# A hybrid block's output projection in seven products: channel tiles regrouped, two products moved forward

## Chip, cores and metric

The kernel runs on one core of one Trainium2 chip. The metric is the device time of one execution in microseconds. The kernel before takes 801.48 us, the median of three runs (801.42 to 801.86).

## What is computed

Input is x, 512 tokens by 2048 channels, in fp32. A norm and an input projection feed eight attention heads (stick-breaking weights) and eight recurrent channel groups (a scan along the tokens), each gated. Their outputs are sixteen channel tiles of 128 channels by 512 tokens, the matrix y. What the change touches is the last step:

```python
y = concat(attention * gate_a, scan * gate_r)        # (512, 2048)
out = x + y @ w_out                                   # w_out (2048, 2048)
```

## The kernel before

**Stages.** Four passes (p = 0 to 3) run three groups of the input projection each: queries and keys, the recurrent inputs, then values and attention gates (vg). Each pass finishes two heads and two recurrent groups. A finished channel tile k goes to a DRAM buffer, y_dram, by a DMA on the sync engine's queue (SP); tiles 0 to 7 are heads, 8 to 15 recurrent groups. The last four to be finished (6, 7, 14 and 15) stay in SBUF as pairs in late[k] and are multiplied out when they are needed (L566, L570). finish_vg(3, ...) is the end of the attention of heads 6 and 7.

**The output projection** is a Strassen-Winograd product. y is cut into four blocks: a11, a21 are the first and second 256 tokens of one half of the channel tiles, a12, a22 those of the other half; w_out is cut in four alike. Seven products p1 to p7 of 256 tokens by 1024 channels by 1024 columns take the place of eight. In the kernel before, the two channel halves are the even and the odd pairs: tile index k = 8b + 2a + s, where s = 0 is the first half, so that a11 holds tiles 0, 2, 4, ..., 14 and needs the late tiles 14 and 6.

**A product** (product(), L592) has two column halves m of 512 columns and, in each, four channel tiles a (two 128-channel tiles, one for each b), so eight slices. A slice takes 12 matmuls of 128x512: each fp32 operand is split into a high and a low fp32r part, and three of the four partial products are summed. The split of a weight tile is a cast on ACT (L608) and a subtraction on DVE (L609), the split of a tile of y the same (L586, L587, first half m = 0 only). The weight splits wo go through three buffers in turn, so a cast waits until the matmuls on the buffer's last contents are done.

**The weights** are four sums or single blocks of w_out, held in tiles of 512 KB. load_c (L549) loads one, as a DMA on SP's queue. add_c (L553) adds another block to a tile in place: a DMA with accum_op add on the queue of the POOL engine (the software queue q0). Both kinds, and the loads of x for the residual (load_res, L630, 256 KB, issued by ACT), run on the same 16 DMA engines. The order of products is p1, p3, p5, p7, p2, p6, p4. The set c1 is loaded, used by p1, and accumulated into after each of its splits (add_to), so that p5, p6 and p4 find the next sum there. The set c2 is loaded with one block, used by p3 as it is, accumulated into during p3, and used by p7, the fourth product. A third set, c3, is loaded for p2. s3, s5, s6 and s7 are sums of blocks of y, made on DVE; e1 is a copy of p1.

**What sets the order.** Within an engine the instructions run in a fixed order, which the tile framework's scheduler made from the program when the kernel was built; the queues of SP, ACT and POOL hold their DMAs in that order too, so an instruction that waits holds up those behind it. Each DMA also waits until an earlier DMA that used the same completion semaphore (there are eight for SP and ACT together, and eight for POOL) has landed.

Of the kernel before, what the change touches and what calls it, by code (L numbers as in the profile page):

```python
# [8 lines left out]
F32 = mybir.dt.float32  # L9
# [12 lines left out]
def hybrid_block_kernel(ctx: ExitStack, tc: tile.TileContext, x, norm_gain, w_in, q_norm_gain,  # L22
# [513 lines left out]
    for tag, cols in ((["c1_1_3", 1024], ["c1_1_2", 1024], ["c1_1_1", 1024], ["c1_1_0", 1024], ["s3", 1024],  # L536
# [3 lines left out]
        slots[tag] = cols  # L540
# [4 lines left out]
    w_out_a = w_out[0].rearrange("(b a s p) (h m n) -> s p a b h m n", p=P, s=2, a=NA, h=2, n=512)  # L545
    y_dram_a = y_dram.rearrange("(b a s) p t -> p a b s t", s=2, a=NA)
# [10 lines left out]
    ya = [held[f"ya{a}"].rearrange("p (b s t) -> p b s t", b=2, s=2) for a in range(NA)]  # L557
    c1 = {(m, a): held[f"c1_{m}_{a}"].rearrange("p (b n) -> p b n", b=2) for m in range(2) for a in range(NA)}
# [5 lines left out]
    for k in (14, 15):  # L564
        y, gate = late[k]
        nc.vector.tensor_tensor(out=ya[3][:, 1, k - 14], in0=y, in1=gate, op=ALU.mult)  # L566
    finish_vg(3, banks, wts)
    for k in (6, 7):
        y, gate = late[k]
        nc.vector.tensor_tensor(out=ya[3][:, 0, k - 6], in0=y, in1=gate, op=ALU.mult)  # L570
# [3 lines left out]
    mixer.close()
    heads.close()
    c2_pool = ctx.enter_context(tc.tile_pool(name="c2", bufs=8, reuse_waits="tile"))
    sa_pool = ctx.enter_context(tc.tile_pool(name="sa", bufs=4, reuse_waits="tile"))
    r_pool = ctx.enter_context(tc.tile_pool(name="res", bufs=4, reuse_waits="tile"))
    ps_o = ctx.enter_context(tc.tile_pool(name="ps_o", bufs=4, space=bass.MemoryType.PSUM,
                                          reuse_waits="tile"))  # L580

    def split_s(i, a, src):
        t = held.pop(f"s{a}") if i == 1 else op_tile(f"s{a}", F32R, f"os{i}_{a}")
# [6 lines left out]
    turn = iter(range(1000))  # L590

    def product(i, pool, tag, src, w, after=None):  # L592
# [4 lines left out]
        for m in range(2):  # L597
            for u in range(2):
                out[m, u] = pool.tile([P, 512], F32, tag=tag, name=f"p{i}_{m}{u}")
            for a in range(NA):  # L600
                if m == 0:
                    s.append(split_s(i, a, src[a]))
                sh, sl = s[a]
                n = next(turn)
                wt = held.pop(f"wo{n}") if n < 3 else op_tile(f"wo{n % 3}", F32R, f"wo{i}_{m}{a}")
                wt = wt.rearrange("p (x b n) -> p x b n", x=2, b=2)
                wh, wl = wt[:, 0], wt[:, 1]
                nc.scalar.copy(wh, w[m, a])  # L608
                nc.vector.tensor_tensor(out=wl, in0=w[m, a], in1=wh.bitcast(F32), op=ALU.subtract)  # L609
# [9 lines left out]
        return out  # L619

# [18 lines left out]
    def tt(out, in0, in1, op=ALU.add, eng=None):  # L639
        (eng or nc.vector).tensor_tensor(out=out, in0=in0, in1=in1, op=op)  # L640
# [4 lines left out]
    a11 = [t[:, :, 0, 0:256] for t in ya]  # L645
    a21 = [t[:, :, 0, 256:512] for t in ya]
    a12 = [t[:, :, 1, 0:256] for t in ya]
    a22 = [t[:, :, 1, 256:512] for t in ya]

    def c2_tile(name):  # L650
        return c2_pool.tile([P, 2, 512], F32, tag="c2", name=name)

    p1 = product(1, ps_mm, "mm", a11, c1, add_to(c1, 0, 1))
    c2 = {(m, a): load_c(c2_tile(f"c2_{m}_{a}"), 1, 1, m, a) for m in range(2) for a in range(NA)}
# [87 lines left out]
```

## Time and profile before

| | us |
|---|---|
| median of three runs | 801.48 (801.42, 801.48, 801.86) |
| profiled execution, its own time | 799.62 |
| its span on the core | 797.9 |
| mean granted clock | 0.987 |
| TensorE (PE) busy | 770.3 (97%) |
| DVE busy | 512.4 (64%) |
| ACT busy | 441.1 (55%) |
| POOL busy | 42.3 (5%) |

All rows below are of the profiled execution, with times from the start of its span. The output projection takes the part from 617 us on. PE busy is a share of the whole span; the stages have different limits, so the rows below are read by stage. A number in square brackets at the end of a row is the time that the engine stood idle before it, and what ended that time. Matmul ends are modelled, so starts are used here.

### The profile page before, as it was taken

How to read it: one execution, taken by the hardware profiler on the slowest of the kernel's cores; microseconds unless marked ns; L12 is line 12 of the kernel's file. 1: busy time of each engine (PE TensorE's matmuls, PEld its weight loads, DVE VectorE, ACT ScalarE, POOL GpSimd, SP SyncE). 2: the span in 40 equal slices, each digit the busy share in tenths (PEclk: the TensorE clock that was granted, in tenths of full speed). 3: DMA queues.
4: the chain of work that ended last, by engine and by line, in shares of the span. 5: the costliest groups of instructions: out<-in, count | busy, mean ns of one | idle time of the engine just before them, and what ended most of it. 6: DMA issues, size and time to landing. Idle time of an engine off the chain costs nothing.

```text
span 797.9 us, 10584 instructions
## 1 busy us (share of the span) xinstructions
PE 770.3 (97%) x3847; PEld 650.6 (82%) x3847; DVE 512.4 (64%) x857; ACT 441.1 (55%) x828; POOL 42.3 (5%) x55
## 2 busy tenths in 40 slices
PE   8999999999999999999999999999998848999997
PEld 7888889888888988888889988888987637888886
DVE  3664578782446787535478782446787916876694
ACT  5835578652356858334578752356857405454451
POOL 0000000000000000000000000000000314410220
PEclk9999999999999999999999999999999888999999
DMA  9622322233232222332322333222245999994591
GB/s 292 198 80 80 106 74 71 95 109 117 81 104 80 87 93 87 119 106 80 106 79 72 101 111 102 93 93 80 80 133 175 273 275 226 198 219 137 116 236 71
DMA packets 82680, 100.35 MB, mean 126 GB/s; under 512 B 5234, under 2 KB 61124, under 8 KB 82628
## 3 DMA queue, kind: packets, MB, share of 16 engines
q1 hardware_dynamic: 71620, 78.70, 31.2%
q0 software_dynamic: 8704, 16.78, 11.9%
q10 hardware_dynamic: 2304, 4.20, 1.5%
q8 instruction: 30, 0.49, 0.3%
q14 instruction: 22, 0.18, 0.1%
HBM read 92.32 MB, written 7.34 MB: 125 GB/s over the span
## 4 chain that ended last, share of the span: by engine, by line
PE 92%; DMA 5%; DVE 1%; issue 0%; SPq 0%; ACT 0%; DVEq 0%
PE p L616 6%; PE p L617 6%; PE p L618 6%; PE z L360 4%; DMA c<-in_w_out_dram 3%; PE qk0b L282 2%; PE qk0b L283 2%; PE xg0b L283 2%; PE qk0b L284 2%; PE xg1b L284 2%; PE xg2b L284 2%; PE xg3b L284 2%; PE xg0b L284 2%; PE xg3b L282 2%; PE xg1b L282 2%; PE xg2b L282 2%
## 5 line engine op out<-in xcount | busy, mean ns | idle before, releaser
L616 PE MATMUL p<-wo,os 128*128 128x512 f32 x192 | 67.5, 394 | 12.5 <-ACT wo L608 12.5
L617 PE MATMUL p<-wo,os 128*128 128x512 f32 x192 | 75.6, 394 | 0.0
L618 PE MATMUL p<-wo,os 128*128 128x512 f32 x192 | 75.4, 393 | 0.0
L616 PEld LDWEIGHTS p<-wo,os 128*128 128x128 f32 x192 | 36.5, 190 | 20.4 <-ACT wo L608 12.9
L608 ACT CAST wo<-c 128x1024 fp32r<-128x1024 f32 x24 | 25.2, 1050 | 45.0 <-PE p L618 29.1
L609 DVE TENSOR_TENSOR wo<-c,wo 128x1024 fp32r<-128x1024 f32 x24 | 29.4, 1224 | 32.0 <-ACT wo L608 31.9
L617 PEld LDWEIGHTS p<-wo,os 128*128 128x128 f32 x192 | 36.4, 190 | 8.3 <-DVE wo L609 0.8
L618 PEld LDWEIGHTS p<-wo,os 128*128 128x128 f32 x192 | 36.5, 190 | 7.6
L372 ACT ACTIVATE sp<-z 128x128 f32<-128x128 f32 (+3 forms) x32 | 13.9, 434 | 25.1 <-PE z L360 24.9
L283 PE MATMUL qk0b<-xl,hqk 128*128 128x512 f32 x64 | 26.4, 413 | 0.0
L284 PE MATMUL qk0b<-xh,lqk 128*128 128x512 f32 x64 | 25.2, 394 | 0.0
L283 PE MATMUL xg0b<-xl,hxg 128*128 128x512 f32 x64 | 25.2, 394 | 0.0
L282 PE MATMUL xg2b<-xh,hxg 128*128 128x512 f32 x64 | 25.1, 393 | 0.0
L282 PE MATMUL xg1b<-xh,hxg 128*128 128x512 f32 x64 | 25.1, 393 | 0.0
L282 PE MATMUL xg3b<-xh,hxg 128*128 128x512 f32 x64 | 25.1, 393 | 0.0
L282 PE MATMUL xg0b<-xh,hxg 128*128 128x512 f32 x64 | 25.1, 392 | 0.0
L283 PE MATMUL xg1b<-xl,hxg 128*128 128x512 f32 x64 | 25.1, 392 | 0.0
L283 PE MATMUL xg3b<-xl,hxg 128*128 128x512 f32 x64 | 25.1, 392 | 0.0
L283 PE MATMUL xg2b<-xl,hxg 128*128 128x512 f32 x64 | 25.1, 392 | 0.0
L284 PE MATMUL qk1b<-xh,lqk 128*128 128x512 f32 x64 | 25.0, 390 | 0.0
L282 PE MATMUL qk2b<-xh,hqk 128*128 128x512 f32 x64 | 24.9, 389 | 0.0
L282 PE MATMUL qk3b<-xh,hqk 128*128 128x512 f32 x64 | 24.9, 389 | 0.0
(538 smaller groups left out, 2440.2 us busy)
## 6 DMA issues: line engine op xcount, KB each, us to landing
c<-in_w_out_dram SPq DMA_DIRECT2D x16, 512.0 KB, 9.0
qk0r<-in_w_in_dram SPq DMA_DIRECT2D x16, 256.0 KB, 4.9
xg0r<-in_w_in_dram SPq DMA_DIRECT2D x16, 256.0 KB, 2.9
vg0r<-in_w_in_dram SPq DMA_DIRECT2D x16, 256.0 KB, 3.1
qk1r<-in_w_in_dram SPq DMA_DIRECT2D x16, 256.0 KB, 2.9
xg1r<-in_w_in_dram SPq DMA_DIRECT2D x16, 256.0 KB, 2.9
vg1r<-in_w_in_dram SPq DMA_DIRECT2D x16, 256.0 KB, 3.0
qk2r<-in_w_in_dram SPq DMA_DIRECT2D x16, 256.0 KB, 3.2
```

Source lines behind the costliest of these rows:

```text
L282: nc.tensor.matmul(banks[b], lhsT=wh[:, cs], rhs=xh[kt], start=st, stop=False)
L283: nc.tensor.matmul(banks[b], lhsT=wh[:, cs], rhs=xl[kt], start=False, stop=False)
L284: nc.tensor.matmul(banks[b], lhsT=wl[:, cs], rhs=xh[kt], start=False, stop=sp)
L360: nc.tensor.matmul(o, lhsT=lhsT, rhs=rhs, start=start, stop=stop, skip_group_check=True)
L372: nc.scalar.activation(e, z, AF.Abs)
L608: nc.scalar.copy(wh, w[m, a])
L609: nc.vector.tensor_tensor(out=wl, in0=w[m, a], in1=wh.bitcast(F32), op=ALU.subtract)
L616: nc.tensor.matmul(out[m, u], lhsT=sh[:, j, us], rhs=wh[:, j, :], start=st, stop=False)
L617: nc.tensor.matmul(out[m, u], lhsT=sh[:, j, us], rhs=wl[:, j, :], start=False, stop=False)
L618: nc.tensor.matmul(out[m, u], lhsT=sl[:, j, us], rhs=wh[:, j, :], start=False, stop=sp)
```

## The change

The channel halves are cut another way: k = 8b + 4s + a. The first half (s = 0, buffers ye) is then tiles 0 to 3 and 8 to 11, all finished early and all loaded from y_dram (L570 of the kernel after); the second half (s = 1, buffers yl) is tiles 4 to 7 and 12 to 15, of which yl0 and yl1 are loaded (L603) and yl2 and yl3 are multiplied out from the late tiles (L606). Blocks a11 and a21 both lie in the first half, so p1 (from a11) and p7 (from s7 = a11 - a21) read early tiles alone.

The order of products becomes p1, p7, p5, p3, p6, p2, p4. p7's weights c2 are a sum of two blocks, so each c2 tile is now loaded and accumulated into before p7 (eight loads, then eight accumulations), and is loaded anew twice: reload(c2, 1, 1) after each split of p7 for p3, and reload(c2, 1, 0) after each split of p3 for p2. The set c3 goes, so there are 32 loads of weight tiles where there were 24; the accumulations stay 32. The residual tiles r12, r22 and r11 have e1 subtracted or added ahead of p3 and p2.

The buffers are laid out anew: four c2 tiles (c2_0) stand beside the c1 tiles, so their loads can start early; the other four (c2_1) are in a pool opened when the mixer's pools close. p1's first half of columns uses the two banks of the pool ps_z. wo has two buffers in p1 and three after it.

```diff
-    for tag, cols in ((["c1_1_3", 1024], ["c1_1_2", 1024], ..., ["c1_0_0", 1024], ["ya0", 2048])):
+    for tag, cols in ([(f"yl{a}", 1024) for a in (3, 2, 1, 0)] + [(f"c2_0_{a}", 1024) for a in (3, 2, 1, 0)]
+                      + [("wo1", 2048), ("s3", 1024), ("s2", 1024)]
+                      + [(f"c1_1_{a}", 1024) for a in (3, 2, 1, 0)]
+                      + [("wo0", 2048), ("s1", 1024), ("s0", 1024)]
+                      + [(f"{n}{a}", 1024) for a in (3, 2, 1, 0) for n in ("c1_0_", "ye")]):
...
-    w_out_a = w_out[0].rearrange("(b a s p) (h m n) -> s p a b h m n", p=P, s=2, a=NA, h=2, n=512)
-    y_dram_a = y_dram.rearrange("(b a s) p t -> p a b s t", s=2, a=NA)
+    w_out_a = w_out[0].rearrange("(b s a p) (h m n) -> s p a b h m n", p=P, s=2, a=NA, h=2, n=512)
+    y_dram_a = y_dram.rearrange("(b s a) p t -> s p a b t", s=2, a=NA)
...
     for a in range(NA):
-        if a < 3:
-            for b in range(2):
-                nc.sync.dma_start(ya[a][:, b], y_dram_a[:, a, b])
+        nc.sync.dma_start(ye[a], y_dram_a[0, :, a])
         load_c(c1[0, a], 0, 0, 0, a)
...
     for a in range(NA):
         load_c(c1[1, a], 0, 0, 1, a)
+    for a in range(NA):
+        load_c(c2[0, a], 0, 1, 0, a)
+        add_c(c2[0, a], 1, 1, 0, a)
...
+    p1 = product(1, banks_1, a11, c1, add_to(c1, 0, 1))
+
+    mixer.close()
...
+    for a in range(NA):
+        c2[1, a] = c2_pool.tile([P, 2, 512], F32, tag="c2", name=f"c2_1_{a}")
+        load_c(c2[1, a], 0, 1, 1, a)
+        add_c(c2[1, a], 1, 1, 1, a)
+    wo_count[1] = 3
...
-    p3 = product(3, ps_o, "o", s3, c2, add_to(c2, 0, 1))
...
+    def reload(tiles, s, h):
+        return lambda m, a: load_c(tiles[m, a], s, h, m, a)
+
+    p7 = product(7, banks_mm, s7, c2, reload(c2, 1, 1))
...
+    p5 = product(5, banks_o, s5, c1, add_to(c1, 1, 1))
...
-    p7 = product(7, ps_o, "o", s7, c2)
-    c3 = {(m, a): load_c(c2_tile(f"c3_{m}_{a}"), 1, 0, m, a) for m in range(2) for a in range(NA)}
...
-    p2 = product(2, ps_mm, "mm", a12, c3)
...
+    p3 = product(3, banks_mm, s3, c2, reload(c2, 1, 0))
...
+    p6 = product(6, banks_o, s6, c1, add_to(c1, 1, 0))
...
+    p2 = product(2, banks_mm, a12, c2)
...
     r21 = {}
     for k in MU:
...
         r21[k] = load_res("e1", f"r21_{k[0]}{k[1]}", 1, 0, *k)
         tt(r21[k], r21[k], f[k])
```

Three places of the built order follow; a name such as c1_0_2 is the tile of column half 0 and channel tile 2, and wo7_10 the split of weights of product 7, column half 1, channel tile 0.

POOL's queue of accumulations, kernel before, from its first accumulation on (all that stand ahead of the second product's own):

```order
L553 DMA c1_0_0__6058<-in_w_out_dram 128x2x512
L553 DMA c1_0_1__6053<-in_w_out_dram 128x2x512
L553 DMA c1_0_2__6048<-in_w_out_dram 128x2x512
L553 DMA c1_0_3__6047<-in_w_out_dram 128x2x512
L553 DMA c1_1_0__6044<-in_w_out_dram 128x2x512
L553 DMA c1_1_1__6043<-in_w_out_dram 128x2x512
L553 DMA c1_1_2__6042<-in_w_out_dram 128x2x512
L553 DMA c1_1_3__6041<-in_w_out_dram 128x2x512
L553 DMA c2_0_0_6284<-in_w_out_dram 128x2x512
```

POOL's queue, kernel after, from its third accumulation on:

```order
L554 DMA c1_0_2__6061<-in_w_out_dram 128x2x512
L554 DMA c1_0_3__6059<-in_w_out_dram 128x2x512
L554 DMA c2_0_0__6048<-in_w_out_dram 128x2x512
L554 DMA c2_0_1__6047<-in_w_out_dram 128x2x512
L554 DMA c1_1_0__6055<-in_w_out_dram 128x2x512
L554 DMA c2_0_2__6046<-in_w_out_dram 128x2x512
L554 DMA c2_0_3__6045<-in_w_out_dram 128x2x512
L554 DMA c1_1_1__6054<-in_w_out_dram 128x2x512
L554 DMA c1_1_2__6053<-in_w_out_dram 128x2x512
L554 DMA c1_1_3__6052<-in_w_out_dram 128x2x512
L554 DMA c2_1_0_6298<-in_w_out_dram 128x2x512
L554 DMA c2_1_1_6301<-in_w_out_dram 128x2x512
```

The c2 accumulations, which stood behind all of p1's and were needed by the fourth product, now stand among p1's and are needed by the second product; c2_1_0 is the thirteenth of the queue.

ACT's queue, kernel before, from the cast of p1's last weight tile to the first two casts of the second product (p3); r11, r12 and r22 are residual tiles, os3 the split of a tile of s3:

```order
L608 CAST wo1_13_6268<-c1_1_3__6041 128x1024
L586 CAST os3_0_6334<-s3_0_6301 128x512
L630 DMA r22_01_6640<-in_x_dram 128x512
L630 DMA r22_10_6644<-in_x_dram 128x512
L630 DMA r22_11_6648<-in_x_dram 128x512
L630 DMA r11_00_6948<-in_x_dram 128x512
L630 DMA r11_01_6953<-in_x_dram 128x512
L608 CAST wo3_00_6337<-c2_0_0_6284 128x1024
L586 CAST os3_1_6353<-s3_1_6307 128x512
L630 DMA r11_10_6958<-in_x_dram 128x512
L630 DMA r11_11_6963<-in_x_dram 128x512
L608 CAST wo3_01_6356<-c2_0_1_6286 128x1024
```

ACT's queue, kernel after, from the middle of p1's second half to its last weight cast:

```order
L647 DMA r22_01_6657<-in_x_dram 128x512
L647 DMA r11_01_6660<-in_x_dram 128x512
L647 DMA r12_10_6663<-in_x_dram 128x512
L647 DMA r22_10_6667<-in_x_dram 128x512
L647 DMA r11_10_6670<-in_x_dram 128x512
L647 DMA r12_11_6673<-in_x_dram 128x512
L581 CAST wo1_12_6249<-c1_1_2__6053 128x1024
L581 CAST os7_0_6333<-s7_0_6310 128x512
L647 DMA r22_11_6677<-in_x_dram 128x512
L647 DMA r11_11_6680<-in_x_dram 128x512
L581 CAST wo1_13_6265<-c1_1_3__6052 128x1024
```

The twelve residual loads, of which five stood directly ahead of the second product's first cast, now all stand ahead of the cast of p1's last weight tile.

ACT's queue, kernel after, between the two column halves of p7:

```order
L581 CAST wo7_03_6393<-c2_0_3__6045 128x1024
L647 DMA r21_00_6980<-in_x_dram 128x512
L647 DMA r21_01_6988<-in_x_dram 128x512
L581 CAST wo7_10_6411<-c2_1_0_6298 128x1024
L581 CAST wo7_11_6427<-c2_1_1_6301 128x1024
```

The loads r21_00 and r21_01 go into the buffers of e1, so each waits for the DVE addition (f) that reads e1 and p7's finished first half; before, they stood ahead of the last cast of p7, wo7_13.

## Rows read from the trace of the kernel before

**Rows 1.** Page, part 4 (share of the longest chain by engine):
```profile
PE 92%; DMA 5%; DVE 1%; issue 0%; SPq 0%; ACT 0%; DVEq 0%
```

**Rows 2.** PE's timeline in the output projection (start, us, what, [idle before]):
```profile
616.94 1.22 PE L616 MATMUL p<-wo__6055,s__6056 128*128 128x512 f32 x2 [3.04 <-ACT wo__6055 L608]
...
625.94 0.50 PE L617 MATMUL p<-wo__6051,s__6052 128*128 128x512 f32 x1 [1.47 <-DVE wo__6051 L609]
...
647.42 0.39 PE L618 MATMUL p<-wo,s__6045 128*128 128x512 f32 x1
660.29 1.22 PE L616 MATMUL p<-wo,os 128*128 128x512 f32 x2 [12.48 <-ACT wo L608]
...
787.83 0.62 PE L616 MATMUL p<-wo,os 128*128 128x512 f32 x2
...
790.55 0.62 PE L616 MATMUL p<-wo,os 128*128 128x512 f32 x2
...
793.04 0.39 PE L618 MATMUL p<-wo,os 128*128 128x512 f32 x1
```

**Rows 3.** Windows: stretch, length, busy us of each engine, PEclk, DMA share, GB/s:
```profile
660.29:793.45 133.16, 133.10 (x576) 109.23 (x576) 99.56 (x118) 62.12 (x72) 28.88 (x24) 0.98 0.79 173
610.00:630.00 20.00, 13.48 (x52) 10.05 (x50) 20.00 (x33) 12.47 (x19) 2.54 (x2) 0.83 0.95 254
595.00:600.00 5.00, 5.00 (x29) 4.31 (x28) 1.39 (x2) 2.08 (x4) 0.00 (x0) 1.00 0.97 353
605.00:610.00 5.00, 5.00 (x34) 4.55 (x33) 4.21 (x10) 4.24 (x9) 0.00 (x0) 1.00 0.01 3
624.00:661.00 37.00, 21.22 (x87) 15.55 (x85) 18.55 (x25) 10.13 (x13) 8.43 (x7) 0.87 1.08 269
660.00:665.00 5.00, 4.67 (x11) 3.23 (x12) 4.40 (x5) 4.65 (x8) 2.41 (x2) 0.53 1.02 294
670.00:700.00 30.00, 30.00 (x134) 24.86 (x133) 25.11 (x32) 14.19 (x16) 13.06 (x11) 1.00 1.12 198
```

**Rows 4.** Chain that ended last, 626 to 661 us (start, us, what):
```profile
628.32 24.65 DMA c<-in_w_out_dram
652.98 0.02 issue
653.00 6.16 DMA r<-in_x_dram
659.16 0.03 issue
659.19 1.05 ACT wo L608
```

**Rows 5.** ACT's timeline, 634 to 660 us (ACTq: time spent issuing DMAs):
```profile
634.88 0.38 ACTq L630 DMA_DIRECT2D r<-in_x_dram  x1
...
637.37 5.39 ACTq L630 DMA_DIRECT2D r<-in_x_dram  x2
642.88 1.05 ACT L608 CAST wo<-c__6041 128x1024 fp32r<-128x1024 f32 x1 [5.34 <-DMA c<-in_w_out_dram]
...
647.69 11.40 ACTq L630 DMA_DIRECT2D r<-in_x_dram  x5
```

**Rows 6.** SP's timeline: the second and third c1 loads, the c2 loads:
```profile
590.88 0.47 SPq L549 DMA_DIRECT2D c__6053<-in_w_out_dram  x1
...
609.65 0.37 SPq L549 DMA_DIRECT2D c__6048<-in_w_out_dram  x1
...
614.75 16.39 SPq L549 DMA_DIRECT2D c<-in_w_out_dram  x8
```

**Rows 7.** POOL's timeline of DMA issues:
```profile
631.17 1.20 POOL L553 DMA_DIRECT2D c__6048<-in_w_out_dram  x1 [3.77 <-DMA c<-in_w_out_dram]
```

**Rows 8.** DVE's timeline: the late tile's product, a weight split, the last sum:
```profile
627.62 0.68 DVE L566 TENSOR_TENSOR ya__6057<-hl,vgl 128x512 f32<-128x512 f32 x1
...
629.42 1.21 DVE L609 TENSOR_TENSOR wo__6049<-c__6048,wo__6049 128x1024 fp32r<-128x1024 f32 x1
...
793.47 0.69 DVE L640 TENSOR_TENSOR r<-p,r 128x512 f32<-128x512 f32 x1 [0.44 <-PE p L618]
```

**Rows 9.** DMA issues, 746 to 749 us: queue, KB each, us to landing:
```profile
c__6058<-in_w_out_dram POOLq DMA_DIRECT2D x1, 512.0 KB, 6.8
```

**Rows 10.** DMA issues and queues' shares, 619 to 647 us:
```profile
q1 hardware_dynamic: 2422, 4.67, 54.7%
q0 software_dynamic: 1168, 2.26, 43.7%
...
c<-in_w_out_dram SPq DMA_DIRECT2D x5, 512.0 KB, 29.0
...
c__6042<-in_w_out_dram POOLq DMA_DIRECT2D x1, 512.0 KB, 20.7
```

More of the change, by code (lines that the diff above doesn't have):

```diff
@@ L556, in hybrid_block_kernel, with two, split @@
     held = {tag: op_tile(tag, F32R if tag[0] in "sw" else F32, f"{tag}_") for tag in slots}
-    ya = [held[f"ya{a}"].rearrange("p (b s t) -> p b s t", b=2, s=2) for a in range(NA)]
-    c1 = {(m, a): held[f"c1_{m}_{a}"].rearrange("p (b n) -> p b n", b=2) for m in range(2) for a in range(NA)}
+    def two(tag):
+        return held[tag].rearrange("p (b n) -> p b n", b=2)
+    ye = [two(f"ye{a}") for a in range(NA)]
+    yl = [two(f"yl{a}") for a in range(NA)]
+    c1 = {(m, a): two(f"c1_{m}_{a}") for m in range(2) for a in range(NA)}
+    c2 = {(0, a): two(f"c2_0_{a}") for a in range(NA)}
+    a11, a21 = [t[:, :, 0:256] for t in ye], [t[:, :, 256:512] for t in ye]
+    a12, a22 = [t[:, :, 0:256] for t in yl], [t[:, :, 256:512] for t in yl]
     for a in range(NA):
-        if a < 3:
-            for b in range(2):
-                nc.sync.dma_start(ya[a][:, b], y_dram_a[:, a, b])
+        nc.sync.dma_start(ye[a], y_dram_a[0, :, a])
         load_c(c1[0, a], 0, 0, 0, a)
[L564 to L570, printed above, removed]
     for a in range(NA):
         load_c(c1[1, a], 0, 0, 1, a)
[L574 to L583, printed above, removed]
+    for a in range(NA):
+        load_c(c2[0, a], 0, 1, 0, a)
+        add_c(c2[0, a], 1, 1, 0, a)
+    def split(t, src):
         t = t.rearrange("p (x b n) -> p x b n", x=2, b=2)
@@ L588, in split_s, with split_w_out, product @@
         return h, l
-    turn = iter(range(1000))
-    def product(i, pool, tag, src, w, after=None):
+    def split_s(i, a, src):
+        return split(held.pop(f"s{a}") if i == 1 else op_tile(f"s{a}", F32R, f"os{i}_{a}"), src)
+    wo_count = [0, 2]
+    def split_w_out(i, m, a, src):
+        n = wo_count[0] % wo_count[1]
+        wo_count[0] += 1
+        if n == 2:
+            return split(wo_pool.tile([P, 2048], F32R, tag="wo", name=f"wo{i}_{m}{a}"), src)
+        return split(held.pop(f"wo{n}") if f"wo{n}" in held else op_tile(f"wo{n}", F32R, f"wo{i}_{m}{a}"), src)
+    ready = {("s", a): split_s(1, a, a11[a]) for a in range(NA)}
+    for a in range(2):
+        ready["w", 0, a] = split_w_out(1, 0, a, c1[0, a])
+    finish_vg(3, banks, wts)
+    for a in range(2):
+        nc.sync.dma_start(yl[a], y_dram_a[1, :, a])
+    for k in (14, 6, 15, 7):
+        y, gate = late[k]
+        nc.vector.tensor_tensor(out=yl[k % 4][:, k // 8], in0=y, in1=gate, op=ALU.mult)
+    def product(i, banks, src, w, after=None):
         out = {}
@@ L619, in product, with banks_mm, banks_1 @@
         return out
+    def banks_mm(m, name):
+        return ps_mm.tile([P, 512], F32, tag="mm", name=name)
+    def banks_1(m, name):
+        return banks_mm(m, name) if m else ps_z.tile([P, 512], F32, tag="z", name=name)
     def res(tag, name):
@@ L637, in hybrid_block_kernel, with tt @@
     MU = [(m, u) for m in range(2) for u in range(2)]
[L639 to L640 removed]
+    def tt(out, in0, in1, op=ALU.add):
+        nc.vector.tensor_tensor(out=out, in0=in0, in1=in1, op=op)
     def add_to(tiles, s, h):
         return lambda m, a: add_c(tiles[m, a], s, h, m, a)
[L645 to L654, printed above, removed]
+    p1 = product(1, banks_1, a11, c1, add_to(c1, 0, 1))
+    mixer.close()
+    c2_pool = ctx.enter_context(tc.tile_pool(name="c2", bufs=4, reuse_waits="tile"))
+    wo_pool = ctx.enter_context(tc.tile_pool(name="wo", bufs=1, reuse_waits="tile"))
+    sa_pool = ctx.enter_context(tc.tile_pool(name="sa", bufs=4, reuse_waits="tile"))
+    r_pool = ctx.enter_context(tc.tile_pool(name="res", bufs=4, reuse_waits="tile"))
+    for a in range(NA):
[3 more added lines that the diff above has]
+    wo_count[1] = 3
     s7, s3 = [], []
@@ L707, in hybrid_block_kernel @@
         tt(r21[k], r21[k], f[k])
-    p4 = product(4, ps_mm, "mm", a22, c1)
+    p2 = product(2, banks_mm, a12, c2)
+    for k in MU:
+        tt(r11[k], p2[k], r11[k])
+        store(r11[k], 0, 0, *k)
+    p4 = product(4, banks_o, a22, c1)
     for k in MU:
```

56 lines of the change are left out of this document (25 added, 31 removed), and 3 rows, old and new, of the table slots.

## The prediction, made before the kernel after was run

> **What bounds the kernel now.** The shares of the longest chain come first: PE makes 92% of it and DMA 5% [rows 1], so the kernel is TensorE work with one or two holes in which it waits for transfers. PE's timeline shows where: p1 starts at 616.94 after 3.04 us of idling, has small waits for the weight splits (1.47 us the largest) and issues its last matmul at 647.42; the second product, p3, starts at 660.29 after 12.48 us in which PE does nothing [rows 2]. From there PE is busy 133.10 of 133.16 us to its end [rows 3]. The chain of waits through the hole is a DMA of c2 of 24.65 us, a residual load r of 6.16 us, then the cast of a weight tile on ACT [rows 4]; ACT spends 11.40 us on issuing five residual loads that stand ahead of that cast [rows 5]. Below that lies the shared resource. From 624 to 661 us the 16 DMA engines are full (share 1.08) at 269 GB/s, and from 605 to 610 they are empty (3 GB/s) [rows 3]. So the hole is bandwidth that comes too late, and the order in which things queue for it.
>
> **What follows the second product needs no new account.** A slice takes 790.55 - 787.83 = 2.72 us [rows 2], a product 8 x 2.72 = 21.8. PE ends at 793.04 + 0.39 = 793.4 [rows 2], so the second product ended at 793.4 - 5 x 21.8 = 684.6, and the span ended 4.5 us behind PE. Five more products follow in the changed kernel too, with operands that are reloaded or accumulated a full product ahead (8 transfers of at most 2.65 us, below, are 21.2 us against 21.8). The whole question is when the second product, now p7, ends: the change in time is that moment less 684.6.
>
> **What the change removes.** p1 and p7 no longer need the late tiles, so p1 starts 1 or 2 us earlier and its short waits shrink; and SP's c1 loads from the third on, which were issued at 609.65 [rows 6] when the projection's last buffers came free, now lie in slots that are free earlier and fill the empty stretch. By themselves these would bring p1's end from 647.8 to about 645. I give this no gain in the sum, because p7 then waits for something else.
>
> **What it adds: accumulations ahead of the second product.** p3 read c2 as it was loaded; p7 reads a sum. Its second column half starts with c2_1_0, the thirteenth accumulation of POOL's queue. The price of one, from the stretch 670 to 700 us, where accumulations alone move with the DMA share at 1.12, is 0.524 MB / 198 GB/s = 2.65 us; a plain load of the same tile costs 0.524 / 353 = 1.49 us in the stretch 595 to 600, and a residual tile half of that, 0.74 [rows 3]. Two accumulations can be over by the time the third (c1_0_2) is issued. That one was issued at 631.17 [rows 7], behind a subtraction that started at 629.42 [rows 8] on a DVE that was busy 20.00 of 20 us [rows 3]; five instructions of about 0.6 us fewer stand ahead of it in the new order, so I take 628. At that time the early plain loads (20 x 1.49 = 30 us from about 592, since the second c1 load was issued at 590.88 [rows 6]) are through.
>
> What must then pass the DMA engines before c2_1_0 is complete: eleven accumulations, 11 x 2.65 = 29.2 us; two loads, c2_1_2 and c2_1_3, which wait for buffers that the last late tile frees at about 628 (its product starts at 627.62 [rows 8]), 3.0; twelve residual tiles, all moved into p1 on ACT's queue, 12 x 0.74 = 8.9; the four reloads of c2_0, issued in p7's first half though nobody needs them until p3, 6.0; and r21_00 and r21_01, 1.5. The sum is 48.6 us for 12.6 MB, or 259 GB/s; at the 269 GB/s that the mixed stretch showed [rows 3] it would be 46.8. A lone accumulation lands 6.8 us after its issue [rows 9], of which 2.65 are transfer, so up to 4 us pass at the start, partly filled by the two loads. c2_1_0 is then complete between 676 and 681 us; I take 679.
>
> **From there to the end of p7.** The cast takes 1.05 [rows 4], the subtraction behind it lets PE run some 0.7 us later, and four slices take 10.9: 691.6. PE has stood idle before that, and after the last such hole it was granted 0.53 of its clock, the 1.2 GHz level, over 660 to 665 us [rows 3], which cost about 2 us: 693.5. The later accumulations of c2_1 follow at 2.65 us against slices of 2.72, so they add nothing unless the reloads of c2_1 mix in. So p7 ends 693.5 - 684.6 = 8.9 us later than p3 did. Against the profiled execution that is 799.62 + 8.9 = 808.5; this execution lies 1.86 us under the median of 801.48, so the prediction is **810.4 us**.
>
> The ends. If the reloads and r21 all come behind c2_1_0 (7.5 us less) and the clock costs nothing, p7 ends at 684.1 and the time is 801.0. If instead the reloads of c2_1 get between the last accumulations (3 x 1.49 = 4.5 us) and everything takes 8% more than the ledger (4 us), it is 819.
>
> **Where else it could wait.** Between p7's halves ACT must issue r21_00 and r21_01, which wait for additions that read p7's finished half, before it may cast wo7_10. Cost with no other wait: 0.69 us for the addition [rows 8], 0.38 for the issue, 1.05 for the cast [rows 5], 0.7 for the subtraction, 2.8 us of idle PE. In my sum it is covered by the wait for c2_1_0; without that wait it stands on the path. The extra subtractions and copies on DVE and ACT are covered: both are mostly idle once p1 runs (DVE was busy 18.55 of 37 us [rows 3]).
>
> **Rivals.**
>
> *The transfers keep pace* and p7 follows p1 directly: 645 + 21.8 + 2.8 = 669.6, 15 us better, 786.5 us. For it speaks that the loads start earlier. Against it, c2_1_3 would have to be complete by 663, and fourteen accumulations from 628 take 37.1 us with nothing beside them, which ends at 665 at the earliest. Chance 0.07.
>
> *An accumulation beside plain loads costs no more than a load* (1.49 us, the nearest row at the other end): this is the case that ends on the faster side. It saves 11 x 1.16 = 12.8 us, c2_1_0 is complete at 666 and p7 ends at about 680, 4.5 us better: 797. The point from which it decides is 2.2 us an accumulation (11 x 0.45 = 5 us less, with no clock lost and half the reloads behind). For it: with all queues loaded, 43.7% of the engines' time in q0 went with 2.26 MB, and 54.7% in q1 with 4.67 MB [rows 10], which is a ratio of 1.65 a byte, a little under the 1.78 of the ledger. Against it: the ratio is not 1, and 198 GB/s was measured with nothing else to move. Chance 0.14. The Trainium skill (DMA: Bandwidth & Descriptors, section "Anatomy of one DMA — SWDGE (gpsimd) path") fits a DMA of this queue by 2.0 us plus its bytes over 436e3, which is an estimate of 1.2 us of transfer for one of these; by it this rival would win and the time would be about 794. The trace disagrees for accumulations: 2.65 us apart, and 6.8 us for a lone one.
>
> *The ledger's lean end*: reloads and r21 fall behind what p7 needs, time about 801 (799 to 804). Chance 0.15.
>
> *ACT stalls first.* The casts of p1's last two weight tiles stand behind ten and twelve residual loads, each of which waits for an earlier DMA on its semaphore, two of them for the loads c2_1_2 and c2_1_3. Loads of that kind landed 29.0 us after issue [rows 10], here 657. POOL's queue is in order: the accumulations into c1_1_2 and c1_1_3 wait for those splits, and c2_1_0 to c2_1_3 stand behind them. If the last cast comes before about 665 the ledger covers it; at 671 every accumulation behind is 6 us late and the time is 817. For it: ACT held 11.40 us on five such loads [rows 5]. Against it: SP has only two loads left at that time, where eight were queued [rows 6]. Chance 0.12.
>
> **How the numbers follow.** My forecast, p7 bound by the accumulations and ending 3 to 14 us later (804 to 815), has 0.52. About 0.2%, or 1.6 us, can be told from no change here. Faster by more: all of the first rival, 0.11 of the second, 0.05 of the lean end, 0.23. Within: 0.03 of the second and 0.06 of the lean end, 0.09. Slower: the rest, 0.68. The range of 796 to 819 leaves out the first rival (0.07), a third of the second and half of the last, 0.18 together.
>
> **What the profile after would show.** Right: PE's first matmul of p7 soon after p1, then a hole of 10 us or more between p7's two halves whose releaser is a DMA of c2 or a cast behind it; DMA share at 1.0 or more from 628 to 680; accumulations landing 10 to 20 us after issue; no hole after p7. Wrong: p7 without a hole of more than 3 us (transfers keep pace); a stretch between 635 and 665 with the DMA share well under 1 while ACT stands on a residual load (ACT stalls first); accumulations landing less than 2.2 us apart among loads (the second rival); or a hole in a later product, which would break the step that five products follow solidly.

## The result: 811.52 us, 1.3% slower, by a wait between the two halves of p7

The changed kernel takes 811.52 us (810.30 to 813.54, four runs), the kernel before 801.45 on the same chip (801.19 to 801.86): a ratio of 1.0128, interval 1.0105 to 1.0151. Its profiled execution took 810.3 us, with a span of 808.6 at a mean granted clock of 0.978.

PE's timeline of the changed kernel, every period of more than 1.3 us in which it waits in the output projection; then the first slice of p5, and the last matmul:

```profile
614.79 0.73 PE L627 MATMUL p<-wo__6056,s__6058 128*128 128x512 f32 x2 [1.49 <-ACT wo__6056 L581]
617.68 0.80 PE L628 MATMUL p<-wo__6056,s__6058 128*128 128x512 f32 x1 [2.16 <-DVE wo__6056 L582]
...
643.36 1.22 PE L627 MATMUL p<-wo,s__6051 128*128 128x512 f32 x2 [5.50 <-ACT wo L581]
...
653.06 0.72 PE L627 MATMUL p<-wo,os 128*128 128x512 f32 x2 [2.14 <-ACT wo L581]
655.18 0.80 PE L628 MATMUL p<-wo,os 128*128 128x512 f32 x1 [1.40 <-DVE wo L582]
...
680.36 1.22 PE L627 MATMUL p<-wo,os 128*128 128x512 f32 x2 [11.87 <-ACT wo L581]
...
693.54 0.62 PE L627 MATMUL p<-wo,os 128*128 128x512 f32 x2
...
803.25 0.39 PE L629 MATMUL p<-wo,os 128*128 128x512 f32 x1
```

The one hole of 12.48 us ahead of the second product [rows 2] is gone, and in its place stand three: 5.50 us inside p1 at 643.36, 2.14 and 1.40 at p7's start, and 11.87 between p7's halves. p7 ends at 693.54, where p5's first slice starts. Behind that PE waits for nothing any more.

The chain that ended last, around the long hole (start, us, what), and ACT's timeline:

```profile
649.14 30.02 DMA c<-in_w_out_dram
...
679.26 1.05 ACT wo L581
```

```profile
635.53 6.64 ACTq L647 DMA_DIRECT2D r<-in_x_dram  x4
642.26 1.04 ACT L581 CAST wo<-c__6053 128x1024 fp32r<-128x1024 f32 x1 [8.24 <-issue]
...
650.96 0.59 ACT L681 COPY e<-p 128x512 f32<-128x512 f32 x1 [0.54 <-PE p L629]
...
651.96 1.05 ACT L581 CAST wo<-c__6048 128x1024 fp32r<-128x1024 f32 x1
...
668.07 1.51 ACTq L647 DMA_DIRECT2D r<-in_x_dram  x2
679.26 1.04 ACT L581 CAST wo<-c 128x1024 fp32r<-128x1024 f32 x1 [16.32 <-DMA c<-in_w_out_dram]
```

The DMA of 30.02 us is the accumulation into c2_1_0, issued at 649.14 and complete at 679.16. The two r21 loads (668.07) are over long before, so their order on ACT costs nothing here. The 5.50 us inside p1 come from four residual loads on which ACT stood for 6.64 us before it could cast p1's seventh weight tile. p7's first tile is cast at 651.96, behind a copy of p1's result that waited for PE.

What held ACT in the 6.64 us is the eighth residual load: it was issued at 640.83, when an earlier load on its semaphore, that of c2_1_3, had landed at 640.81.

The windows (columns as in [rows 3]) show the shared resource and the clock:

```profile
605.00:610.00 5.00, 5.00 (x31) 4.44 (x30) 4.38 (x9) 4.26 (x10) 0.00 (x0) 1.00 1.03 333
628.00:680.00 52.00, 31.41 (x116) 23.79 (x114) 26.13 (x35) 13.35 (x17) 16.45 (x14) 0.78 1.06 253
680.00:685.00 5.00, 4.61 (x11) 3.21 (x12) 2.45 (x2) 1.99 (x3) 0.00 (x0) 0.56 1.12 208
693.54:803.64 110.10, 110.10 (x481) 89.91 (x479) 78.53 (x93) 48.77 (x55) 18.05 (x15) 1.00 0.70 154
```

The stretch from 605 to 610, empty before at 3 GB/s [rows 3], now moves 333 GB/s: the loads do start earlier, and p1 starts at 614.79 where it was 616.94. But from 628 to 680 the DMA engines are full for 52 us and move 13.14 MB. After the hole PE was granted 0.56 of its clock, near the 1.2 GHz level, as after the hole of before (0.53).

How long each accumulation took, from the rows of POOL's issues (start) and of DMA issues from 628 to 680 us (KB each, us to landing):

```profile
627.34 1.20 POOL L554 DMA_DIRECT2D c__6061<-in_w_out_dram  x1 [5.25 <-DVE wo L582]
...
648.41 1.20 POOL L554 DMA_DIRECT2D c__6052<-in_w_out_dram  x1 [2.34 <-DVE wo L582]
```

```profile
c__6061<-in_w_out_dram POOLq DMA_DIRECT2D x1, 512.0 KB, 7.5
...
c__6052<-in_w_out_dram POOLq DMA_DIRECT2D x1, 512.0 KB, 26.6
```

Start plus landing time gives 634.8 for c1_0_2, 675.0 for the last one ahead of c2_1_0, and c2_1_0 follows at 679.2. From c1_0_2 to c2_1_0 ten steps take 44.3 us: the accumulations land about 4.4 us apart while loads move beside them. What each kind costs the engines is in the row of POOL's queue in the same 52 us (packets, MB, share of the engines' time):

```profile
q0 software_dynamic: 3262, 6.30, 66.4%
```

The other queues moved the remaining 6.84 MB in 39.7%, so a byte of an accumulation took 1.8 times as long as a byte of a load. The prediction's prices, 2.65 and 1.49 us, have a ratio of 1.78.

**Where the 10.7 us of span went.** The boundary at the end of the second product lies at 693.54 now. In the kernel before it lay at 684.47, the start of its third product, so it moved by 9.07:

```profile
684.47 0.62 PE L616 MATMUL p<-wo,os 128*128 128x512 f32 x2
```

From there PE takes 803.25 + 0.39 - 693.54 = 110.10 us, against 793.04 + 0.39 - 684.47 = 108.96 before: 1.14. The end behind PE takes 4.96 instead of 4.47: 0.5.

### The profile page after: what moved, and what is told of

Same layout as the page of the kernel before. It is cut to its first block, busy times and chain, and to the rows that moved or that the text cites. A ratio compares the mean times of both kernels' runs of the same rounds, so it can differ in the third digit from the quotient of the medians.

```text
span 808.6 us, 10599 instructions
## 1 busy us (share of the span) xinstructions
PE 774.3 (96%) x3847; PEld 652.3 (81%) x3847; DVE 512.5 (63%) x857; ACT 441.2 (55%) x828; POOL 42.6 (5%) x55
## 4 chain that ended last, share of the span: by engine, by line
PE 90%; DMA 5%; issue 2%; POOL 2%; DVE 0%; SPq 0%; ACT 0%; POOLq 0%; ACTq 0%; DVEq 0%
PE p L627 5%; PE p L628 5%; PE p L629 5%; DMA c<-in_w_out_dram 4%; PE z L360 4%; PE qk0b L283 2%; PE qk0b L284 2%; PE xg0b L283 2%; PE xg3b L284 2%; PE xg1b L284 2%; PE xg2b L284 2%; PE xg0b L284 2%; PE xg1b L282 2%; PE xg2b L282 2%; PE xg3b L282 2%
## 5 line engine op out<-in xcount | busy, mean ns | idle before, releaser
L627 PE MATMUL p<-wo,os 128*128 128x512 f32 x192 | 68.9, 401 | 14.0 <-ACT wo L581 14.0
L628 PE MATMUL p<-wo,os 128*128 128x512 f32 x192 | 77.1, 402 | 1.4 <-DVE wo L582 1.4
L629 PE MATMUL p<-wo,os 128*128 128x512 f32 x192 | 76.6, 399 | 0.0
L628 PEld LDWEIGHTS p<-wo,os 128*128 128x128 f32 x192 | 37.1, 193 | 10.7 <-DVE wo L582 2.6
L581 ACT CAST wo<-c 128x1024 fp32r<-128x1024 f32 x12 | 12.6, 1049 | 35.2 <-DMA c<-in_w_out_dram 21.6
L582 DVE TENSOR_TENSOR wo<-c,wo 128x1024 fp32r<-128x1024 f32 x12 | 14.7, 1224 | 22.2 <-ACT wo L581 20.6
```

Of the source, the lines that this page charges most:

```text
L627: nc.tensor.matmul(out[m, u], lhsT=sh[:, j, us], rhs=wh[:, j, :], start=st, stop=False)
L628: nc.tensor.matmul(out[m, u], lhsT=sh[:, j, us], rhs=wl[:, j, :], start=False, stop=False)
L629: nc.tensor.matmul(out[m, u], lhsT=sl[:, j, us], rhs=wh[:, j, :], start=False, stop=sp)
```

## Experiments

Each batch ran beside the kernel before on its own chip, and ratios are to that; chips differ by some 0.2% (799.85, 800.07 and 801.64 us for the kernel before, against 801.45 above), so ratios are compared, not times. The line numbers of edited kernels are shifted by a few. issue_after places an instruction behind another in the built order.

**The theory** is the prediction's: what p7 needs is queued behind 48.6 us of transfers, and c2_1_0 completes when those have passed. **The rival** is ACT's queue: the casts stand behind residual loads, and the weights are not the cause.

### The accumulations that nobody needs yet go last

```diff
-    p1 = product(1, banks_1, a11, c1, add_to(c1, 0, 1))
+    p1 = product(1, banks_1, a11, c1)
...
-        add_c(c2[1, a], 1, 1, 1, a)
+        last_c2 = add_c(c2[1, a], 1, 1, 1, a)
+    with tc.issue_after(last_c2.ins):
+        for m in range(2):
+            for a in range(NA):
+                add_c(c1[m, a], 0, 1, m, a)
```

> The eight accumulations into c1 that p1 issues are queued behind the eight into c2 on POOL, nothing else is changed. Queue theory (p7's second half waits for what stands ahead of c2_1_0 in the DMA queues): c2's tiles are all complete by about 650 us, p7 follows p1 without a hole of over 3 us and ends near 675; c1's sums then come at 2.65 us each, as fast as p5 uses them; time 789 to 796 us, below the kernel before. Rival (the hole comes from ACT's order, the residual loads and the r21 loads ahead of the casts, or from the price of an accumulation wherever it stands): the hole stays or goes to p5 in full, time 808 to 814.

Measured: 798.16 us, ratio 0.9974 (0.9961 to 0.9987). PE's timeline from 640 us on, its waits ahead of p1's seventh slice, of p7 and of p7's second half (two more, of 0.27 and 0.54 us, follow the first two):

```profile
645.09 0.99 PE L627 MATMUL p<-wo,s__6051 128*128 128x512 f32 x2 [4.70 <-ACT wo L581]
...
654.90 0.72 PE L627 MATMUL p<-wo,os 128*128 128x512 f32 x2 [2.14 <-ACT wo L581]
...
669.08 0.50 PE L628 MATMUL p<-wo,os 128*128 128x512 f32 x1 [0.28 <-DVE wo L582]
```

The same bytes in another order, and the hole of 11.87 us is gone. What is left of the changed kernel's holes are the 4.70 us inside p1, again behind four residual loads on ACT (6.23 us there), and the start of p7. With them p1 ended at 652.8 and p7 at 679.8, where the forecast had 675, and the time is 2 us above the forecast range. The build moved one thing more: ACT's two r21 loads stand behind p7's sixth and seventh weight casts here, not ahead of the fifth. In the changed kernel they held nothing (above), so the long hole was not theirs.

### The second block of the sum left out

```diff
     for a in range(NA):
         load_c(c2[0, a], 0, 1, 0, a)
-        add_c(c2[0, a], 1, 1, 0, a)
...
         load_c(c2[1, a], 0, 1, 1, a)
-        add_c(c2[1, a], 1, 1, 1, a)
```

> The eight accumulations into c2 are left out, so p7 and all that uses it are made from one block of w_out in place of the sum of two. Queue theory: p7 waits for plain loads alone, which land by 641 us; it follows p1's end (650) with no hole but the 2.8 us for r21 between its halves, and ends at about 675; time 789 to 793 us. If that hole is wider than 2 us the price of r21's place is shown; if p7 runs without it, that term of the prediction falls. Rival (it is the reloads and residual loads that are late): a hole of 10 us stays, time above 800.

Measured: 789.77 us (one run), with p7's weights one block instead of the sum of two. From 630 us on PE waits once, 3.96 us inside p1 for ACT, and p7 follows p1 without a hole:

```profile
642.52 1.22 PE L626 MATMUL p<-wo,s__6051 128*128 128x512 f32 x2 [3.96 <-ACT wo L580]
```

So it is the sum of c2, made ahead of its first use, that p7 waits for. In this build the r21 loads came later in ACT's order, so the bubble of 2.8 us that the prediction priced for them stays untested. p7's first weight cast came earlier, ahead of the copies of p1's result, and p7 starts without a wait.

### One term of the ledger at a time

Two kernels take single terms away from in front of c2_1_0: all residual tiles (12 x 0.74 and r21's 1.5, 10.4 us), and the four reloads of c2_0 (6.0 us).

```diff
     def load_res(tag, name, i, j, m, u):
...
-        nc.scalar.dma_start(t, x2[ts, ns])
+        with tc.issue_after(last_p5.ins):
+            nc.scalar.dma_start(t, x2[ts, ns])
```

> The twelve residual loads, and with them r21, are queued on ACT behind p5's last cast; nothing else is changed. Queue theory: 12 x 0.74 = 8.9 us of transfer fewer ahead of c2_1_0, which lands at about 670 instead of 679.2, and p1's 5.5 us hole ahead of its seventh slice goes; p7 ends near 685, time 801 to 804 us. Rival (ACT stalls first): p1's hole goes and c2_1_0 is issued earlier, but lands at 677 or later, because the eleven accumulations take 4 us each whatever stands beside them; time 808 to 811.

```diff
-    p7 = product(7, banks_mm, s7, c2, reload(c2, 1, 1))
+    def second_half(m, a):
+        if m == 1:
+            again = load_c(c2[1, a], 1, 1, 1, a)
+            if a == NA - 1:
+                with tc.issue_after(again.ins):
+                    for i in range(NA):
+                        load_c(c2[0, i], 1, 1, 0, i)
+
+    p7 = product(7, banks_mm, s7, c2, second_half)
```

> The four reloads of c2_0 are queued on SP behind the last reload of c2_1, so none stands in the DMA queues ahead of c2_1_0; nothing else is changed. Queue theory: 4 x 1.49 = 6.0 us of transfer fewer, c2_1_0 lands at about 673 instead of 679.2 and p7 ends about 6 us earlier; time 803 to 806 us. Rival (an accumulation beside other transfers takes 4 us by itself): c2_1_0 lands at 677 or later; time 808 to 811.

The chain's row of c2_1_0 and PE's row behind it, without the residual tiles, then without the reloads:

```profile
644.42 24.89 DMA c<-in_w_out_dram
...
670.50 1.22 PE L629 MATMUL p<-wo,os 128*128 128x512 f32 x2 [8.95 <-ACT wo L581]
```

```profile
650.39 23.23 DMA c<-in_w_out_dram
...
674.81 1.22 PE L626 MATMUL p<-wo,os 128*128 128x512 f32 x2 [5.69 <-ACT wo L580]
```

c2_1_0 is complete at 669.31 and 673.62. The measure that is free of what comes earlier is the time from the issue of c1_0_2's accumulation to that moment:

| kernel | issue | c2_1_0 complete | us between | less than 51.8 | ledger's term |
|---|---|---|---|---|---|
| after | 627.34 | 679.16 | 51.8 | | |
| residual tiles later | 628.12 | 669.31 | 41.2 | 10.6 | 10.4 |
| reloads of c2_0 later | 628.67 | 673.62 | 45.0 | 6.8 | 6.0 |

Both terms come out at their price within 1 us. With no residual tile beside them the accumulations land closer together: start plus landing time is 642.4 for c2_0_0 and 652.6 for c2_0_3, four steps of 2.5 us. In time the second kernel gained: 805.06 us (one run), where theory said 803 to 806. The first did not: 812.42 us, ratio 1.0165 (1.0144 to 1.0186). ACT's timeline of that kernel shows why, and PE's row behind it:

```profile
698.45 13.06 ACTq L650 DMA_DIRECT2D r<-in_x_dram  x12
...
712.08 1.04 ACT L581 CAST wo<-c__6048 128x1024 fp32r<-128x1024 f32 x1
```

```profile
713.17 1.22 PE L629 MATMUL p<-wo,os 128*128 128x512 f32 x2 [6.52 <-ACT wo L581]
```

ACT stands 13.06 us on issuing twelve loads, and p3's casts stand behind them. The first eight take 4.3 us; the last four, which share semaphores with the first, go out one by one until 711.5 as those land. The gain in p7 was given back at p3's start (6.52 us, and 2.01 more for the subtraction).

### ACT's queue by itself

Here the residual loads are issued by SP at the same place in the program, in the changed kernel and in the kernel before:

```diff
-        nc.scalar.dma_start(t, x2[ts, ns])
+        nc.sync.dma_start(t, x2[ts, ns])
```

> The kernel after with its residual loads (r21 too) issued by SP instead of ACT. The same bytes stand ahead of c2_1_0 in the DMA engines, while no cast waits behind a residual load. Queue theory: p1's 5.5 us hole goes and p1 ends by 646, but c2_1_0 still lands at 676 to 681 and p7 has a longer hole; time 807 to 812, no gain. If ACT's order was what made p7 late, the hole goes and the time is 790 to 800.

> The kernel before with its residual loads issued by SP instead of ACT, at the same place among SP's DMAs (behind the c2 loads), so that the same bytes move at about the same time and no cast stands behind them. If the hole ahead of p3 was ACT's queue (casts behind loads that wait for their semaphores), it goes: p3 starts within 2 us of p1's end, time 785 to 790 us. If it was bandwidth (c2 late because the residual tiles move too), p3 still waits until 652 or later: 793 to 799.

The changed kernel so edited takes 809.64 us, ratio 1.0106 (1.0079 to 1.0133): the 5.50 us inside p1 are gone and p7 starts at 647.23, but its weights are no earlier. c2_1_0 is cast at 677.95, 49.9 us after the issue at 628.07, and p7 waits in two more places instead. Its last long hole, and the first matmul behind p7:

```profile
679.05 1.22 PE L627 MATMUL p<-wo,os 128*128 128x512 f32 x2 [8.56 <-ACT wo L581]
...
694.26 0.62 PE L627 MATMUL p<-wo,os 128*128 128x512 f32 x2
```

p7 ends at 694.26, where p5 starts; it was 693.54. So in the changed kernel ACT's queue is not what decides p7's end.

The kernel before, so edited, takes 796.91 us, ratio 0.9949 (0.9936 to 0.9962). PE's timeline has no wait between 631.41 and 676.86, so the hole of 12.48 us ahead of p3 [rows 2] is gone with the same bytes in flight. The time missed its forecast of 785 to 790 all the same. What comes instead, on PE and on DVE:

```profile
676.86 0.79 PE L617 MATMUL p<-wo,os 128*128 128x512 f32 x1 [10.24 <-DVE wo L609]
```

```profile
672.92 0.69 DVE L640 TENSOR_TENSOR r<-r,e 128x512 f32<-128x512 f32 x1 [11.54 <-DMA r<-in_x_dram]
...
675.59 1.22 DVE L609 TENSOR_TENSOR wo<-c,wo 128x1024 fp32r<-128x1024 f32 x1
```

DVE waits for a residual tile with a subtraction of weights queued behind that addition. A late residual load holds PE either way, at its issue on ACT or at its use on DVE.

### The residual loads later, and then one at a time, in the kernel before

```diff
-        nc.scalar.dma_start(t, x2[ts, ns])
+        with tc.issue_after(last_p3.ins):
+            nc.scalar.dma_start(t, x2[ts, ns])
```

> The kernel before, with its residual loads queued on ACT behind the last cast of its second product p3. If the hole of 12.48 us was half the residual loads' (6.16 us in the chain of waits, and their share of the DMA engines), p3 starts at 650 to 654 instead of 660.3 and the time falls to 791 to 795 us. If the c2 loads alone set it, p3 starts at 654 or later, 795 to 797. If the time goes elsewhere (p5 then waits for the accumulations that p3 issues), 800.

```diff
-        r12[k] = load_res("r12", f"r12_{k[0]}{k[1]}", 0, 1, *k)
+        r12[k] = load_res("r12", f"r12_{k[0]}{k[1]}", 0, 1, *k, cast[3, 0, 2 * k[0] + k[1]])
...
-        r22[k] = load_res("r22", f"r22_{k[0]}{k[1]}", 1, 1, *k)
+        r22[k] = load_res("r22", f"r22_{k[0]}{k[1]}", 1, 1, *k, cast[5, 0, 2 * k[0] + k[1]])
...
-        r11 = load_res("r11", f"r11_{k[0]}{k[1]}", 0, 0, *k)
+        r11 = load_res("r11", f"r11_{k[0]}{k[1]}", 0, 0, *k, cast[7, 0, 2 * k[0] + k[1]])
```

(The last argument is the cast behind which the load is issued.)

> The kernel before, with its residual loads queued one at a time behind the casts of the first halves of p3, p5 and p7. The hole of 12.48 us ahead of p3 goes as in e6_before_residuals_late, and the 4.92 us wait in its p5, which came from residual loads that landed late, goes too: p3 starts within 2 us of p1's end and no hole follows; 4 to 6 us better than e6_before_residuals_late, 787 to 791 us. Rival (the accumulations that p3 issues become the bound of p5 or p7 once p3 starts 12 us earlier): a wait for a DMA of c in p5 or p7, 793 to 797. If it is as fast as e7_c1_late_residuals_spread, the new order of products earns nothing by itself.

All twelve behind p3's last cast: 794.16 us, ratio 0.9930 (0.9907 to 0.9953), p3 follows p1 without a hole, and p5 waits 4.92 us at 691.34 behind additions that wait for residual tiles. One at a time: 785.99 us, ratio 0.9832 (0.9808 to 0.9855), the fastest kernel of this study and 1 us better than its forecast. After 630 us its PE waits once:

```profile
696.63 0.50 PE L618 MATMUL p<-wo,os 128*128 128x512 f32 x1 [1.61 <-DVE wo L610]
```

### The same for the new order

This kernel has the c1 accumulations behind c2's, as in the first experiment, and the residual loads one at a time behind casts of p7, p5 and p3; it also has the third weight buffer moved (next section).

> The kernel after with three edits: c1's accumulations of p1 queued behind c2's (as in e1_c1_adds_late), the residual loads queued one at a time behind the casts of p7's second half, p5's first and p3's first, and the third weight buffer moved (as in e5_wo_moved). Queue theory: nothing that p7 needs is late, and ACT holds no cast behind a residual load: p1 ends by 648, p7 starts within 2.5 us and has no hole, p5 and p3 follow solidly; 5 to 8 us better than e1_c1_adds_late, 788 to 793 us, 1.0 to 1.5% under the kernel before. Rival (moving work only moves the hole): a hole of over 5 us in p5 or p3, time 795 to 800.

Measured: 790.98 us, ratio 0.9889 (0.9871 to 0.9906), so better than the kernel before by 1.1%, but not than the old order with the same care. Its PE waits from 630 us on:

```profile
646.80 0.73 PE L630 MATMUL p<-wo,os 128*128 128x512 f32 x2 [2.14 <-ACT wo L581]
648.06 0.50 PE L631 MATMUL p<-wo,os 128*128 128x512 f32 x1 [0.53 <-DVE wo L582]
...
678.32 0.73 PE L630 MATMUL p<-wo,os 128*128 128x512 f32 x2 [1.59 <-ACT wo L581]
679.58 0.79 PE L631 MATMUL p<-wo,os 128*128 128x512 f32 x1 [0.53 <-DVE wo L582]
```

These are 4.79 us, against 1.61 in the old order. Windows of 640 to 660 and 680 to 690 us:

```profile
640.00:660.00 20.00, 17.28 (x67) 13.15 (x66) 12.88 (x16) 8.78 (x11) 11.10 (x9) 0.91 1.06 207
680.00:690.00 10.00, 10.00 (x39) 8.06 (x39) 8.89 (x12) 3.96 (x4) 4.77 (x5) 0.85 1.09 287
```

In both stretches, each with waits, the granted clock is 0.91 and 0.85 (a part of each at the 1.2 GHz level); in the old order with spread loads it is 1.00 in both. That costs, as an estimate, 17.28 x 0.09 + 10 x 0.15 = 3.1 us more. Waits and clock together are 3.2 + 3.1 = 6.3 us, near the 6.4 between the two spans (789.3 and 782.9). The agreement is rough, since it leaves out 0.9 us that the new order is ahead at p1's last matmul (644.27 against 645.22) and 0.5 that it loses behind PE's end.

One step further, with two copies of p1 (e1) on ACT put behind casts of p7 and the residual loads a product later:

> e7_c1_late_residuals_spread with two more edits: the copies of p1's second half (e1) are queued on ACT behind p7's third and fourth weight casts instead of ahead of the first, and the residual loads stand one product later (r12 and r22 behind p3's casts, r11 behind p6's). If the holes that e7 still had (2.14 us ahead of p7, 1.59 us in p5) came from ACT's order, both go and the new order of products runs solid from p1 on: 4 to 5 us better than e7, 785 to 788 us, level with e8_before_residuals_spread. If the accumulations bound p7 after all, the holes stay or move and the time stays at 789 to 792.

Measured: 796.34 us, ratio 0.9936 (0.9918 to 0.9955), a miss. The wait at p7's start shrank to 1.66 us but did not go, because another cast stands ahead of p7's first weights on ACT, the split of a tile of s7, which waits for p1's last matmuls too:

```profile
646.99 0.62 ACT L581 CAST os<-s 128x512 fp32r<-128x512 f32 x1 [2.45 <-PE p L632]
```

The wait in p5 went, and p3 and p6 wait instead, behind additions on DVE that wait for residual tiles (2.40 us the longest). One of them, on PE and on DVE:

```profile
734.70 0.50 PE L631 MATMUL p<-wo,os 128*128 128x512 f32 x1 [1.59 <-DVE wo L582]
```

```profile
732.82 0.69 DVE L661 TENSOR_TENSOR r<-r,e 128x512 f32<-128x512 f32 x1 [3.08 <-DMA r<-in_x_dram]
```

That loads came too late for their additions is shown. The span is 5.8 us longer than that of the kernel it builds on (795.1 and 789.3): p3 takes 5.2 us more and p6 2.8, and p5 gives 4.3 back. p7 starts 1.8 later, although its own wait shrank, because p1 ends 2.3 us later. That part lies ahead of what was edited, and its cause was not looked for.

### Where the 1.14 us in the last five products come from

In the kernel after, of every three slices one takes longer; the weight buffers go round in threes. The edit puts an unused tile of 1152 bytes a partition ahead of the third buffer, which moves it from offset 39776 to 40928. The other two lie at 180192 and 147424, and by steps of 8192 bytes all three then have the same remainder (8160). So have the three buffers of the kernel before (196576, 172000 and 155616), where the slices behind the second product take 2.72 us. The edit moves the tiles that lie behind the third buffer by the same 1152 bytes (s7, s3, e1, f and the residual tiles).

```diff
+    pad_pool = ctx.enter_context(tc.tile_pool(name="pad", bufs=1, reuse_waits="tile"))
+    pad_pool.tile([P, 288], F32, tag="pad", name="pad")
```

> An unused tile of 1152 bytes a partition stands ahead of the third weight-split buffer, so that its place in SBUF has the same remainder by 8192 bytes as the other two; nothing else is changed. If the 2.79 to 2.80 us slices after p7 (every third one, against 2.72) come from where that buffer lies, all slices take 2.72 us and the 40 slices after p7 take 1.0 us less; if from its being the third buffer or from a load that falls there, every third slice stays at 2.79. The hole in p7 stays as it was; time 808 to 812.

Slice starts on PE, kernel after and then with the buffer moved:

```profile
696.26 0.62 PE L627 MATMUL p<-wo,os 128*128 128x512 f32 x2
...
699.06 0.63 PE L627 MATMUL p<-wo,os 128*128 128x512 f32 x2
...
701.79 0.61 PE L627 MATMUL p<-wo,os 128*128 128x512 f32 x2
```

```profile
695.93 0.61 PE L627 MATMUL p<-wo,os 128*128 128x512 f32 x2
...
698.65 0.61 PE L627 MATMUL p<-wo,os 128*128 128x512 f32 x2
...
701.37 0.61 PE L627 MATMUL p<-wo,os 128*128 128x512 f32 x2
```

After: 2.80, then 2.73 (and 2.72 from 693.54, above). Moved: 2.72 each, in all 40 slices, and the last five products take 108.96 us again, as in the kernel before. The time, 811.56 us (one run), shows no gain, since c2_1_0 came later in that execution (p7's hole is 12.08 us there and ends at 682.71); the slices are the verdict here, not the time. Why the place matters was not tried.

## Why the prediction was right, and where it was not

The prediction was 810.4 us, the result 811.52, inside the range, on the side given 0.68, and by the mechanism forecast.

- **What p7 waits for.** c2_1_0 complete at 679.16, forecast 679. That it agrees to 0.2 us is partly luck: the sum gives 628 + 48.6 = 676.6, and the rest of the range up to 681 was left open for the start. The terms are better evidence: the removal of single terms gave 10.6 and 6.8 us where the ledger had 10.4 and 6.0, and putting c2's accumulations first, or leaving them out, removed the hole. That settles the first rival (transfers keep pace), the second and the lean end: by them PE would have had no such hole, or c2_1_0 would have been complete at 666, or the reloads would not have counted. The second rival needed a byte of an accumulation to cost no more than a byte of a load; beside loads it cost 1.8 times as much (q0's row above). The Trainium skill (DMA: Bandwidth & Descriptors, section "Anatomy of one DMA — SWDGE (gpsimd) path") has 2.0 us plus the bytes over 436e3 for a DMA of POOL's queue, an estimate of 1.2 us of transfer for one of these; the trace disagrees for accumulations, which took twice that even at 2.5 us apart. One sign was set too narrow: the accumulations landed 7.5 to 32 us after their issue, not 10 to 20.
- **From there to p7's end.** 693.54 - 679.16 = 14.4 us, forecast 14.5; the granted clock was 0.56 behind the hole, forecast 0.53.
- **The term that was mis-sized**: "five more products follow" at an unchanged 2.72 us a slice. No wait came, as forecast, but the new layout put one weight buffer where a slice takes up to 2.80: 1.14 us over 40 slices. The end behind PE added 0.5, without a cause shown. Together they are 1.6 of the 1.8 us between a span forecast 8.9 us longer and one 10.7 longer.
- **"ACT stalls first"** happened, and did not decide. I gave p1's end as 645 and it was 650.9 (650.53 for its last matmul), for the 5.50 us that the cast of its seventh tile waited for ACT. The rival put the landing of c2_1_3's load, on which ACT waits, at 657; it came at 640.8, so p1's last cast was well ahead of 665 and the ledger covered the stall, as the rival's condition said. With the loads on SP p7 started 5.8 us earlier and ended 0.7 later (694.26).
- **p7's own start** was priced at nothing, and costs 2.14 + 1.40 us here: ACT casts its first tile only after the copies of p1's result (650.96 above) and the split of s7's last tile, which wait for p1's last matmuls. With two of the copies out of the way 1.66 us were left; where the build put the cast itself ahead (the sum left out) there was no wait. In the kernel after, the long hole hides it; with that gone it is on the path (2.14 us in the first experiment and in the best version of the new order).
- **The step that was wrong** is the reading of before: "the hole is bandwidth that comes too late, and the order in which things queue for it". It names the residual loads on ACT, but takes them for a part of the queue for bandwidth. The load of c2_0_0 was issued at 614.75 [rows 6] and took 12.8 us to land, so p3's first weights lay ready at 627.5, 20 us ahead of p1's end. The cast stood behind ACT's five residual loads of 11.40 us [rows 5], and those behind earlier DMAs on their semaphores [rows 4]. The row that would have told is that of the issue:

```profile
c<-in_w_out_dram SPq DMA_DIRECT2D x1, 512.0 KB, 12.8
```

Issuing the residual loads on SP, or later on ACT, removed that hole with no byte less. The bandwidth was full and set how long those loads held ACT, but p3's own weights were not late. The Trainium skill (DMA: Bandwidth & Descriptors, the same section) states that a semaphore wait happens on the issuing sequencer, before the transfer is dispatched; the trace agrees, with 11.40, 6.64 and 13.06 us of ACT on issues in front of casts. The misreading did not touch the sum, since the changed kernel's bound was argued by itself, but it hid the better change: spreading twelve loads gains 1.7% (0.9832), and the best version tried of the new order is behind that (0.9889).

What stays open: why a slice depends on the place of its weight buffer, what the r21 loads would cost with nothing to cover them, and why p1 ended later in the last experiment on the new order.

## To carry to other kernels

Before a hole is put down to late data, look up when the data landed; if it lay there, look for what stands in front of the consumer on its own engine, DMA issues above all, since here an issue waited for an earlier transfer's semaphore and held the casts behind it. Issue such loads one at a time between computations, early enough for their use and late enough for their buffers. Where transfers are the bound, add up what is queued ahead of the one that is needed: such a ledger, priced from this kernel's own rows, was right to 1 us in the two terms that were tested. Here putting the needed transfers first was worth more (811.52 to 798.16 us) than starting all of them earlier.

## What the runs showed of the hardware

- The same twelve matmuls took 2.79 to 2.80 us from one weight buffer and 2.72 to 2.74 from two others, and 2.72 from all three when that buffer lay 1152 bytes further on.
- An accumulating DMA of 512 KB landed 2.5 to 2.65 us behind the one before it when few or no loads moved, and 4.4 us when loads moved beside it. Loads and accumulations together then moved 253 GB/s with all engines full, and a byte of an accumulation took 1.8 times as much of the engines' time as a byte of a load.
